# Streaming encoder trunk: the sample block's norm taken apart at the start of each FFN, and the second pair's own-block products issued first

## The chip, the cores and the metric

The kernel runs on one core of one Trainium2 chip. A core has five engines with queues of their own that work in order and meet through semaphores: TensorE (PE in the profile; PEld is its weight load), VectorE (DVE), ScalarE (ACT), GpSimd (POOL) and SyncE (SP), whose queue issues nearly all loads. The metric is the device time of one execution in microseconds (us).

## The reference

One inference step of a two-layer encoder for two groups of requests: a prompt of 512 rows and a sample of 8 x 16 = 128 rows, model width 1024, all float32. Layer 0 mixes with stick-breaking attention and gated linear attention, layer 1 with chunk-band softmax attention. After each mixer comes a norm and a SwiGLU FFN of hidden width 2816. The change lies in the two FFNs:

```python
def _rmsnorm(x, g):
    xf = x.astype(jnp.float32)
    y = xf * lax.rsqrt(jnp.mean(xf * xf, axis=-1, keepdims=True) + EPS)
    return (y * g.astype(jnp.float32)).astype(x.dtype)

def _swiglu(h, wg, wu, wd):
    return (jax.nn.silu(h @ wg) * (h @ wu)) @ wd
...
for layer in range(DEPTH):
    ...
    xp = xp + _swiglu(_rmsnorm(xp, norm_ffn_g[layer]), w_ffn_gate[layer], w_ffn_up[layer], w_ffn_down[layer])
    xs = xs + _swiglu(_rmsnorm(xs, norm_ffn_g[layer]), w_ffn_gate[layer], w_ffn_up[layer], w_ffn_down[layer])
```

## The kernel before

**Rows and columns.** Prompt and sample lie together as 640 rows, five blocks of 128; block 4 is the sample. The input of an FFN is held transposed in four tiles fT (256 columns of the model each, 640 rows). The FFN's rows fall in two halves of 320: n = 0 is blocks 0, 1 and half of 2, n = 1 the rest with the sample. The model's columns fall in two halves as well, so fT has four quarters: b11 and b21 (rows n = 0), b12 and b22 (rows n = 1).

**Products.** Each float32 product is three matmuls on parts of reduced precision: high x high, high x low, low x high. `split` (L286) makes the high part of a weight on ScalarE (`wh`, L289) and the low part on VectorE (`wl`, L290); four buffers of each exist, so splits run at most four products ahead. `product` (L688) is 12 matmuls of 128 x 320 (L692 to L694). `block` (L660) splits an operand in the same way (`xb` for a quarter, `xt` for a combined one; cast L664, difference L665), `comb` (L653) makes the combined operands t1 to t4 from quarters by VectorE differences (`xs`, L657).

**Pairs of matrices.** The FFN walks over the hidden width in groups of 6, 6, 6 and 4 tiles of 128. For every two tiles it takes a slice of the gate weights and then the same slice of the up weights; `fast_pair` (L670) is one such matrix of 1024 x 256, loaded as two halves `raw`. A matrix has four own blocks A. Usually it is computed with seven products in place of eight: `head` (b21 into py, b11 into px), `body` (t3 into pq; t2 on px; b22 into py; t1 on px), `tail` (t4 on pq). For t3, t2, t1 and b22 in the body, `weights` (L697) makes sums of own blocks on GpSimd: s3 and s1 come from own blocks, s2 from s1, s4 from s2. They lie in four buffers `sw`, and are split like weights.

**The start of an FFN.** The first pair (matrices 0 and 1 of group 0, gate and up) is computed plainly, with `part`: part(0) does the rows n = 0 with four products (b11, b21 for two output tiles), part(1) the rows n = 1 (b12, b22). So the first eight products need no sample rows. In the program's order (L779 to L799) stand: blocks b11 and b21, part(0) of matrix 0, part(0) of matrix 1, then `last_norm`, the norm of the sample block, then blocks b12 and b22, both part(1), the head of matrix 2, and the combinations and blocks t3, t1, t2, t4. `last_norm` is `norm_block` (L247) on xt[4]: `rstd_of` (L230) squares both halves of the rows on ScalarE with a sum (`sqj`, L235), takes the root as exp(-0.5 ln) with one correction step (L240 to L244), then both halves are scaled to `h` (L252; the first on VectorE, the second on GpSimd), transposed on TensorE (`tp`, L255) and written into fT with the gain (L261 on VectorE, L263 on ScalarE). The transposes are told to issue only after the last matmul of part(0) of matrix 1.

**What sets the order.** The program does not fix an engine's queue. A planner orders the instructions when the program is built, by their place in the program (or a priority given) and its own estimate of times; buffers of a ring with one tag are handed out by it as well. Six buffers with the tag `ws` serve, in an FFN, the squares' scratch `sqj`, the scaled rows `h`, the gate and up results `sg` and `up`, and the combined operands `xs`.

Of the kernel before, what the change touches and what calls it, by code (L numbers as in the profile page):

```python
# [13 lines left out]
ALU = mybir.AluOpType  # L14
PSUM = bass.MemoryType.PSUM

P = 128
# [38 lines left out]
def kernel(  # L56
# [8 lines left out]
    nc = tc.nc  # L65
# [35 lines left out]
    def tagged(tag, bufs, where="all"):  # L101
        def f(shape, name, dt=F32):
            return pools[where].tile(shape, dt, tag=tag, bufs=bufs, name=name)
        return f
# [5 lines left out]
    ws = tagged("ws", NWS)  # L110
# [12 lines left out]
    def pp(shape, name="pp"):  # L123
        return pps.tile(shape, F32, tag="pp", name=name)

    def za(shape, name="za"):
        return banks["za"].tile(shape, F32, tag="za", name=name)
# [23 lines left out]
    def plain():  # L151
# [14 lines left out]
        out=mask_a, in_=mask_a, pattern=[[-1, P]], compare_op=ALU.is_gt,  # L166
# [23 lines left out]
    def make_gla_masks(ch, nm):  # L190
# [23 lines left out]
        out=rowm, in_=rowm, pattern=[[-DS, DB]], compare_op=ALU.is_ge,  # L214
# [3 lines left out]
        out=rowm, in_=rowm, pattern=[[DS, DB]], compare_op=ALU.is_ge,  # L218
        fill=0.0, base=DS - 1, channel_multiplier=-1,
    )  # L220

    xs_flat = x_sample.rearrange("b t d -> (b t) d")

    def x_rows(src_p, src_s, b):
# [5 lines left out]
    def rstd_of(xt, sb=None):  # L230

        ss = small.tile([P, 2], F32, tag="ss", name="ss")
        for i in range(2):
            j = (sb or ws)([P, 512], "sqj")
            nc.scalar.activation(j, xt[i], AF.Square, scale=1.0 / 32.0, accum_out=ss[:, i:i + 1])  # L235
        v = small.tile([P, 1], F32, tag="rv", name="rv")
        r = small.tile([P, 1], F32, tag="rr", name="rr")
        a = small.tile([P, 1], F32, tag="ra", name="ra")
        V = nc.vector
        V.tensor_scalar(v, ss[:, 0:1], ss[:, 1:2], EPS, op0=ALU.add, op1=ALU.add)  # L240
        nc.scalar.activation(r, v, AF.Ln)
        last_exp[:] = [nc.scalar.activation(r, r, AF.Exp, scale=-0.5)]
        V.tensor_scalar(a, r, r, v, op0=ALU.mult, op1=ALU.mult)
        V.tensor_scalar(r, a, -3.0, r, op0=ALU.add, op1=ALU.mult)  # L244
        return r

    def norm_block(xt, gi, hT, b, sb=None, bank=None, after=None):  # L247
        r = rstd_of(xt, sb)
        for i in range(2):
            tp = (bank or za)([P, 4, P], "tp")  # L250
            h = (sb or ws)([P, 512], "h")
            scaled = (nc.vector, nc.gpsimd)[i].tensor_scalar(h, xt[i], r, -0.5, op0=ALU.mult, op1=ALU.mult)  # L252
            with tc.issue_after(after.ins) if after else nullcontext():
                for j in range(4):
                    nc.tensor.transpose(tp[:, j, :], h[:, j * P:(j + 1) * P], ident)  # L255
            for j in range(4):
                c = 4 * i + j
                if len(hT) == 4:
                    d = hT[c // 2][:, c % 2, b * P:(b + 1) * P]
                    if j % 2:  # L260
                        nc.vector.tensor_scalar(d, tp[:, j, :], gm[:, gi, c:c + 1], None, op0=ALU.mult)  # L261
                    else:
                        nc.scalar.activation(d, tp[:, j, :], AF.Copy, scale=gm[:, gi, c:c + 1])  # L263
                    continue
                H = hT[c][:, 0, b * P:(b + 1) * P]
                L = hT[c][:, 1, b * P:(b + 1) * P]
                g = gm[:, gi, c:c + 1]
                nc.scalar.activation(H, tp[:, j, :], AF.Copy, scale=g)
                nc.vector.scalar_tensor_tensor(
                    L, tp[:, j, :], g, H.bitcast(F32), op0=ALU.mult, op1=ALU.subtract)  # L270
        return scaled

    def new_hT(nm):
        return [t5([P, 2, NT], f"{nm}{c}", F32R) for c in range(8)]
# [395 lines left out]
    def fast_pair(W, c0, X, out):  # L670


        r = [pool.tile([P, 4, 256], F32, tag="raw", bufs=NRAW, name="raw"),
             pools["stage"].tile([P, 4, 256], F32, tag="rawf", bufs=2, name="raw")]
        for k in range(2):
            nc.sync.dma_start(r[k], W[512 * k:512 * k + 512, c0:c0 + 256].rearrange("(k p) n -> p k n", p=P))
        A = [[r[k][:, :, P * m:P * m + P] for k in range(2)] for m in range(2)]

        def part(n):

            for m in range(2):
                ps = za([P, 320], "pb")
                for k in range(2):
                    last = product(ps, A[m][k], (("b11", "b21"), ("b12", "b22"))[n][k], k == 0)
                out(m, n, ps, None)
            return last

        def product(ps, a, x, first=True):  # L688
            H, L = split(a, 4, P)
            for k in range(4):  # L690
                f = dict(skip_group_check=True)
                MM(ps, lhsT=H[:, k, :], rhs=X[x][0][k], start=(first and k == 0), stop=False, **f)  # L692
                MM(ps, lhsT=H[:, k, :], rhs=X[x][1][k], start=False, stop=False, **f)  # L693
                last = MM(ps, lhsT=L[:, k, :], rhs=X[x][0][k], start=False, stop=(k == 3), **f)  # L694
            return last

        def weights(a, b, op):  # L697
            t = sm_([P, 4, P], "sw")
            nc.gpsimd.tensor_tensor(t, a, b, op=op)  # L699
            return t  # L700
        st = {}

        def copy(ps):
            t = u2_([P, 320], "u2")
            nc.scalar.copy(t, ps)
            return t

        def head():
            st["Y"] = Y = pp([P, 320], "py")
            product(Y, A[0][1], "b21")  # L710
            st["X"] = Z = za([P, 320], "px")
            product(Z, A[0][0], "b11")
            st["P"] = copy(Z)

        def body():
            Z = st["X"]
            out(0, 0, st["Y"], st["P"])
            st["Q"] = Q = za([P, 320], "pq")
            s3 = weights(A[0][0], A[1][0], ALU.subtract)
            product(Q, s3, "t3")  # L720
            s1 = weights(A[1][0], A[1][1], ALU.add)
            s2 = weights(s1, A[0][0], ALU.subtract)
            product(Z, s2, "t2", False)
            q7 = copy(Q)
            st["U"] = copy(Z)
            Y = pp([P, 320], "py")
            s4 = weights(A[0][1], s2, ALU.subtract)
            product(Y, s4, "b22")
            product(Z, s1, "t1", False)
            out(0, 1, Z, copy(Y))  # L730
            out(1, 1, Z, q7)

        def tail():
            product(st["Q"], A[1][1], "t4", False)
            out(1, 0, st["Q"], st["U"])
        return head, body, tail, part

    def ffn(l, xt, fT, after, last_norm):
        X, comb, block = operand(fT)
        c0, silu = 0, []  # L740
        for gi, G in enumerate(GROUPS):
            gT, mats = [], []
# [33 lines left out]
            for i, (head, body, tail, part) in enumerate(mats):  # L776
                if gi == 0 and i == 1:
                    continue
                if gi == 0 and i == 0:  # L779


                    block("b11")
                    block("b21")
                    part(0)
                    last_norm(mats[1][3](0))
                    block("b12", gt_)
                    block("b22")
                    part(1)
                    mats[1][3](1)
                    mats[2][0]()  # L790
                    comb("t3", "b22", "b12")
                    block("t3")
                    comb("t1", "b12", "b11")
                    comb("t2", "b22", "t1")
                    block("t2")
                    block("t1")
                    comb("t4", "b21", "t2")
                    block("t4")
                    continue  # L799
                if gi or i > 2:  # L800
                    head()
                if i > 2 * (gi == 0):
                    mats[i - 1][2]()
                body()
            mats[-1][2]()
            if gi == len(GROUPS) - 1:
                with tc.issue_after(silu[-1].ins):
# [20 lines left out]
    hT = new_hT("hTa")  # L828
# [266 lines left out]
    for t in ORDER.split():  # L1095
        step(t)
    hT = new_fT("fT0")
    xt = mixer_end(w_out_ab[0], oT, oS, lambda b: x_rows(x_prompt, xs_flat, b), 1, hT, a_sample,
                   [FIRST + 99500 + 1000 * t for t in WHEN[0]])
# [9 lines left out]
        last_scaled[:] = [norm_block(xt[b], 2, hT2, b)]  # L1109
    stack.close()  # L1110
    with ffn_pools():
        ffn(0, xt, hT, after0, lambda mm: norm_block(xt[4], 1, hT, 4, after=mm))
    hT = hT2


# [53 lines left out]
    for half in range(2):  # L1169
# [7 lines left out]
        for p in range(p0 + 1, p0 + 4):  # L1177
            c_attend(p, *c_pair(p))

    hT = new_fT("fT1")  # L1180
    xt = mixer_end(w_out_c[0], oT, oS, lambda b: xd[b], 3, hT, lambda: (mixer_banks(*BANKS[2]), [c_sample(h) for h in range(2)]),
                   [FIRST + 299500 + 1000 * t for t in WHEN[1]])
# [11 lines left out]
        nc.sync.dma_start(dst, y)  # L1194
    stack.close()
    with ffn_pools():
        ffn(1, xt, hT, after1, lambda mm: norm_block(xt[4], 3, hT, 4, after=mm))


# [37 lines left out]
```

## Time and profile before

| what | value |
|---|---|
| time, median of 3 runs | 1778.29 us (1778.0, 1778.29, 1786.5) |
| the profiled execution: its time | 1781.72 us |
| the profiled execution: its span | 1780.0 us |
| granted clock of TensorE, mean over the span | 0.979 |
| HBM read, written | 175.75 MB, 14.29 MB |
| FFN 0 begins its first product at | 439.8 us |
| FFN 1 begins its first product at | 1321.0 us |

A row of a timeline gives start, duration, engine, line and operation, the tile written and those read, partitions x elements, a count, and in brackets how long the engine had been idle before and what ended that. A wait row gives the waiting line, what it waited for, the total in us, how often, and the longest. L numbers are lines of the kernel before.

### The profile page before, as it was taken

The numbers are of one execution on the slowest core, as the hardware profiler recorded it, in microseconds if no ns is written. First come the engines' busy times: TensorE is split into PE (matmuls) and PEld (weight loads), VectorE is DVE, ScalarE is ACT, GpSimd is POOL, SyncE is SP. The second block draws the span as 40 slices with busy tenths as digits, with TensorE's granted clock in tenths as the row PEclk, the third lists the DMA queues.
The fourth block names the chain that finished last, engine by engine and source line by source line (L and its number), as shares of the span: only waits on it lengthen the run. The fifth ranks groups of instructions, "written<-read, shape, count | busy, mean of one in ns | idle before, by whom it ended". The sixth has DMA issues, their size and how long they took to land.

```text
span 1780.0 us, 31737 instructions
## 1 busy us (share of the span) xinstructions
PE 1697.9 (95%) x12520; PEld 1522.9 (86%) x12520; DVE 1108.4 (62%) x2237; ACT 812.0 (46%) x1805; POOL 317.7 (18%) x339
## 2 busy tenths in 40 slices
PE   7999999998889999999999999999787999999997
PEld 7898997896788998989898889888567889899896
DVE  6466586765684765856555654755647837658465
ACT  6454435455552543534454433534536525335253
POOL 2000000000241413414110000001104224043130
PEclk9999998999899999999999999999998999999999
DMA  5311131574122222222343233368822313222212
GB/s 144 97 56 49 56 97 54 186 244 155 59 77 90 71 96 71 73 95 70 122 134 99 83 96 108 116 211 300 311 98 62 105 60 95 83 83 73 93 60 83
DMA packets 157173, 192.09 MB, mean 108 GB/s; under 512 B 12976, under 2 KB 109248, under 8 KB 157024
## 3 DMA queue, kind: packets, MB, share of 16 engines
q1 hardware_dynamic: 153440, 178.40, 30.8%
q0 software_dynamic: 3584, 11.67, 2.1%
q8 instruction: 98, 1.61, 0.4%
q14 instruction: 51, 0.42, 0.1%
HBM read 175.75 MB, written 14.29 MB: 107 GB/s over the span
## 4 chain that ended last, share of the span: by engine, by line
PE 82%; DVE 11%; ACT 3%; issue 2%; DMA 2%; SPq 0%; DVEq 0%; ACTq 0%
PE pn L323 6%; PE pn L325 6%; PE pn L324 6%; PE pw L304 5%; PE pw L305 5%; PE pw L306 5%; DVE wl L290 3%; PE px L692 3%; PE px L693 3%; PE px L694 3%; PE kttp L535 2%; PE py L694 2%; PE pm L356 2%; PE pm L359 2%; PE pm L358 2%
## 5 line engine op out<-in xcount | busy, mean ns | idle before, releaser
L290 DVE TENSOR_TENSOR wl<-raw,wh 128x512 fp32r<-128x512 f32 (+1 forms) x370 | 289.0, 788 | 251.0 <-ACT wh L289 248.5
L289 ACT CAST wh<-raw 128x512 fp32r<-128x512 f32 (+1 forms) x370 | 227.8, 618 | 377.7 <-PE pn L325 163.4
L699 POOL TENSOR_TENSOR sw<-raw 128x512 f32<-128x512 f32 x80 | 128.5, 1610 | 533.2 <-DMA raw<-in_w_ffn_gate_dram 298.2
L324 PE MATMUL pn<-wl,gT 128*128 128x512 f32 x440 | 171.2, 389 | 0.0
L289 ACT CAST wh<-sw 128x512 fp32r<-128x512 f32 x160 | 99.4, 621 | 154.9 <-PE px L693 64.4
L325 PE MATMUL pn<-wh,gT 128*128 128x512 f32 x440 | 169.3, 389 | 0.0
L323 PE MATMUL pn<-wh,gT 128*128 128x512 f32 x440 | 166.8, 389 | 0.0
L290 DVE TENSOR_TENSOR wl<-sw,wh 128x512 fp32r<-128x512 f32 x160 | 120.7, 758 | 52.6 <-ACT wh L289 41.4
L694 PE MATMUL py<-xb,wl 128*128 128x320 f32 x320 | 100.6, 314 | 9.2 <-DVE wl L290 9.2
L694 PE MATMUL pq<-xt,wl 128*128 128x320 f32 x320 | 98.8, 310 | 4.0 <-DVE wl L290 4.0
L692 PE MATMUL pq<-xt,wh 128*128 128x320 f32 x320 | 99.1, 310 | 2.2 <-ACT wh L289 2.2
L692 PE MATMUL px<-xt,wh 128*128 128x320 f32 x320 | 98.9, 309 | 0.0
L693 PE MATMUL pq<-xt,wh 128*128 128x320 f32 x320 | 98.9, 309 | 0.0
L693 PE MATMUL px<-xt,wh 128*128 128x320 f32 x320 | 98.9, 309 | 0.0
L694 PE MATMUL px<-xt,wl 128*128 128x320 f32 x320 | 98.9, 309 | 0.0
L693 PE MATMUL py<-xb,wh 128*128 128x320 f32 x320 | 98.8, 309 | 0.0
L692 PE MATMUL py<-xb,wh 128*128 128x320 f32 x320 | 98.8, 309 | 0.0
L325 PEld LDWEIGHTS pn<-wh,gT 128*128 128x128 f32 x440 | 82.6, 188 | 16.9
L324 PEld LDWEIGHTS pn<-wl,gT 128*128 128x128 f32 x440 | 82.6, 188 | 16.9
L323 PEld LDWEIGHTS pn<-wh,gT 128*128 128x128 f32 x440 | 82.3, 188 | 16.6
L304 PE MATMUL pw<-hTa,wh 128*128 128x320 f32 (+1 forms) x272 | 89.9, 331 | 0.0
L305 PE MATMUL pw<-hTa,wh 128*128 128x320 f32 (+1 forms) x272 | 88.9, 327 | 0.0
(329 smaller groups left out, 4721.5 us busy)
## 6 DMA issues: line engine op xcount, KB each, us to landing
raw<-in_w_ffn_gate_dram SPq DMA_DIRECT2D x44, 512.0 KB, 3.8
raw<-in_w_ffn_up_dram SPq DMA_DIRECT2D x44, 512.0 KB, 3.7
raw<-in_w_ffn_down_dram SPq DMA_DIRECT2D x44, 512.0 KB, 3.3
kr<-in_cache_c_k_dram SPq DMA_DIRECT2D x64, 256.0 KB, 5.4
vr<-in_cache_c_v_dram SPq DMA_DIRECT2D x16, 1024.0 KB, 7.0
raw<-in_w_in_ab_dram SPq DMA_DIRECT2D x24, 512.0 KB, 3.8
raw<-in_w_qkv_c_dram SPq DMA_DIRECT2D x24, 512.0 KB, 3.8
vr<-in_cache_a_v_dram SPq DMA_DIRECT2D x8, 1024.0 KB, 5.6
```

Source lines behind the costliest of these rows:

```text
L289: nc.scalar.copy(H, rawv)
L290: nc.vector.tensor_sub(L, rawv, H.bitcast(F32))
L304: MM(ps[i], lhsT=H[:, k % 4, :], rhs=hT[k][:, 0, s], start=(k == 0), stop=False)
L305: MM(ps[i], lhsT=H[:, k % 4, :], rhs=hT[k][:, 1, s], start=False, stop=False)
L306: MM(ps[i], lhsT=L[:, k % 4, :], rhs=hT[k][:, 0, s], start=False, stop=(k == 7))
L323: MM(ps[b], lhsT=lhs[k][:, 0, bs], rhs=H, start=(k == 0), stop=False)
L324: MM(ps[b], lhsT=lhs[k][:, 0, bs], rhs=L, start=False, stop=False)
L325: MM(ps[b], lhsT=lhs[k][:, 1, bs], rhs=H, start=False, stop=(k == K - 1))
L692: MM(ps, lhsT=H[:, k, :], rhs=X[x][0][k], start=(first and k == 0), stop=False, **f)
L693: MM(ps, lhsT=H[:, k, :], rhs=X[x][1][k], start=False, stop=False, **f)
L694: last = MM(ps, lhsT=L[:, k, :], rhs=X[x][0][k], start=False, stop=(k == 3), **f)
L699: nc.gpsimd.tensor_tensor(t, a, b, op=op)
```

## The change

`norm_block` is divided in `norm_rows` (square, root, scaling) and `norm_columns` (transposes and the write into fT). In each FFN the rows of the sample block are now asked for ahead of the first products, with both scalings on VectorE; the columns follow part(0) of matrix 0, their transposes behind its last matmul, and part(0) of matrix 1 comes after them. The head of matrix 3 is issued directly behind the head of matrix 2, ahead of the combinations. In the body of matrix 2 the sums s1, s2, s4 and the b22 product come first, and s3 with the t3 product after them. All other uses of the norm keep their order.

```diff
+    ROWS = (nc.vector, nc.vector)
...
-    def norm_block(xt, gi, hT, b, sb=None, bank=None, after=None):
+    def norm_rows(xt, sb=None, engines=None):
+
         r = rstd_of(xt, sb)
+        hs = []
         for i in range(2):
+            h = (sb or ws)([P, 512], "h")
+            scaled = (engines or (nc.vector, nc.gpsimd))[i].tensor_scalar(
+                h, xt[i], r, -0.5, op0=ALU.mult, op1=ALU.mult)
+            hs.append(h)
+        return hs, scaled
+
+    def norm_block(xt, gi, hT, b, sb=None, bank=None):
+        hs, scaled = norm_rows(xt, sb)
+        norm_columns(hs, gi, hT, b, bank)
+        return scaled
+
+    def norm_columns(hs, gi, hT, b, bank=None, after=None):
+
+        for i, h in enumerate(hs):
             tp = (bank or za)([P, 4, P], "tp")
-            h = (sb or ws)([P, 512], "h")
-            scaled = (nc.vector, nc.gpsimd)[i].tensor_scalar(h, xt[i], r, -0.5, op0=ALU.mult, op1=ALU.mult)
             with tc.issue_after(after.ins) if after else nullcontext():
...
-        def body():
+        def body(own=False):
+
             Z = st["X"]
             out(0, 0, st["Y"], st["P"])
             st["Q"] = Q = za([P, 320], "pq")
+            if own:
+                s1 = weights(A[1][0], A[1][1], ALU.add)
+                s2 = weights(s1, A[0][0], ALU.subtract)
+                s4 = weights(A[0][1], s2, ALU.subtract)
+                Y = pp([P, 320], "py")
+                product(Y, s4, "b22")
+                y = copy(Y)
             s3 = weights(A[0][0], A[1][0], ALU.subtract)
             product(Q, s3, "t3")
-            s1 = weights(A[1][0], A[1][1], ALU.add)
-            s2 = weights(s1, A[0][0], ALU.subtract)
+            if not own:
+                s1 = weights(A[1][0], A[1][1], ALU.add)
+                s2 = weights(s1, A[0][0], ALU.subtract)
             product(Z, s2, "t2", False)
             q7 = copy(Q)
             st["U"] = copy(Z)
-            Y = pp([P, 320], "py")
-            s4 = weights(A[0][1], s2, ALU.subtract)
-            product(Y, s4, "b22")
+            if not own:
+                Y = pp([P, 320], "py")
+                s4 = weights(A[0][1], s2, ALU.subtract)
+                product(Y, s4, "b22")
             product(Z, s1, "t1", False)
-            out(0, 1, Z, copy(Y))
+            out(0, 1, Z, y if own else copy(Y))
             out(1, 1, Z, q7)
...
+                    rows = last_norm[0]()
                     block("b11")
                     block("b21")
-                    part(0)
-                    last_norm(mats[1][3](0))
+                    last_norm[1](rows, part(0))
+                    mats[1][3](0)
                     block("b12", gt_)
                     block("b22")
                     part(1)
                     mats[1][3](1)
                     mats[2][0]()
+                    mats[3][0]()
                     comb("t3", "b22", "b12")
...
-                if gi or i > 2:
+                if gi or i > 3:
                     head()
                 if i > 2 * (gi == 0):
                     mats[i - 1][2]()
-                body()
+                body(gi == 0 and i == 2)
...
-        ffn(0, xt, hT, after0, lambda mm: norm_block(xt[4], 1, hT, 4, after=mm))
+        ffn(0, xt, hT, after0, (lambda: norm_rows(xt[4], engines=ROWS)[0],
+                              lambda rows, mm: norm_columns(rows, 1, hT, 4, after=mm)))
...
-        ffn(1, xt, hT, after1, lambda mm: norm_block(xt[4], 3, hT, 4, after=mm))
+        ffn(1, xt, hT, after1, (lambda: norm_rows(xt[4], engines=ROWS)[0],
+                              lambda rows, mm: norm_columns(rows, 3, hT, 4, after=mm)))
```

More of the change, by code (lines that the diff above doesn't have):

```diff
@@ L270, in norm_block @@
                     L, tp[:, j, :], g, H.bitcast(F32), op0=ALU.mult, op1=ALU.subtract)
-        return scaled
     def new_hT(nm):
```

## The prediction

> **What bounds the kernel now.** I read the page first: sections 1 and 4.
>
> ```profile
> PE 1697.9 (95%) x12520; PEld 1522.9 (86%) x12520; DVE 1108.4 (62%) x2237; ACT 812.0 (46%) x1805; POOL 317.7 (18%) x339
> ...
> PE 82%; DVE 11%; ACT 3%; issue 2%; DMA 2%; SPq 0%; DVEq 0%; ACTq 0%
> ```
>
> TensorE sets the time nearly everywhere. The change removes none of its products, so it can gain only where TensorE stands still or runs at a lower granted clock. Next the waits of TensorE, in the stretch where each FFN begins (FFN 0 near 440 us, FFN 1 near 1321 us).
>
> ```profile
> PE tp L255 <- DVE h L252: 5.0, 1, 5.0
> PE pb L693 <- DVE xb L665: 1.9, 1, 1.9
> PE pb L692 <- ACT xb L664: 1.3, 1, 1.3
> ...
> PE tp L255 <- DVE h L252: 4.9, 1, 4.9
> ```
>
> The first three are FFN 0 (454 to 470), the last is FFN 1. After the eight plain products of parts 0, TensorE waits 5 us for the scaled rows of the sample block, then for the low and high parts of what they feed. Windows put a size on it (columns: stretch, its length, busy time and count of PE, PEld, DVE, ACT and POOL, granted clock, DMA share, GB/s).
>
> ```profile
> 439.80:454.50 14.70, 14.70 (x99) 14.07 (x97) 8.15 (x15) 8.06 (x17) 0.00 (x0) 1.00 0.00 1
> 454.50:469.40 14.90, 6.76 (x25) 5.88 (x25) 9.93 (x15) 6.41 (x16) 6.36 (x5) 0.66 0.24 71
> ...
> 481.10:511.20 30.10, 24.75 (x163) 23.70 (x162) 29.37 (x38) 17.81 (x34) 20.63 (x8) 1.00 0.18 54
> ...
> 1335.50:1350.40 14.90, 6.83 (x28) 5.87 (x26) 9.95 (x15) 6.42 (x16) 6.36 (x5) 0.66 0.25 73
> ...
> 1362.00:1392.10 30.10, 24.69 (x163) 23.65 (x162) 29.36 (x38) 17.83 (x34) 20.64 (x8) 1.00 0.18 54
> ```
>
> Two things are to be seen. In 454.5 to 469.4 TensorE has 25 matmuls where the stretch before had 99, at a clock of 0.66. And in 481 to 511 (pair 2's bodies) VectorE has no idle left (29.37 of 30.10) and TensorE loses 5.35 us. The cadence, from the timeline of TensorE:
>
> ```profile
> 439.01 1.04 PE L255 MATMUL tp<-ident,h 128*128 128x128 f32 x8
> 439.80 0.39 PE L692 MATMUL pb<-xb,wh 128*128 128x320 f32 x1
> ...
> 459.57 1.94 PE L255 MATMUL tp<-ident,h 128*128 128x128 f32 x8 [4.95 <-DVE h L252]
> ...
> 466.29 0.47 PE L692 MATMUL pb<-xb,wh 128*128 128x320 f32 x1
> 466.55 0.47 PE L693 MATMUL pb<-xb,wh 128*128 128x320 f32 x1
> ...
> 469.42 0.31 PE L692 MATMUL pb<-xb,wh 128*128 128x320 f32 x1
> 469.56 0.31 PE L693 MATMUL pb<-xb,wh 128*128 128x320 f32 x1
> ```
>
> 0.26 us from one start to the next after the gap, 0.147 at full clock (14.70 / 99 in the stretch before is 0.148). A product of 12 matmuls is 1.76 us.
>
> Why are the rows so late? The timeline of the other engines:
>
> ```profile
> 439.21 0.69 DVE L626 TENSOR_TENSOR x<-x,ps 128x512 f32<-128x512 f32 x1 [6.18 <-PE ps L625]
> ...
> 441.14 2.17 ACT L289 CAST wh<-raw 128x512 fp32r<-128x512 f32 x4
> ...
> 455.03 0.42 ACT L763 COPY up<-pb 128x320 f32<-128x320 f32 x1
> 455.34 0.63 ACT L235 ACTIVATE sqj<-x 128x512 f32<-128x512 f32 x1
> ...
> 458.06 1.36 DVE L252 TENSOR_SCALAR h<-x,rr 128x512 f32<-128x512 f32 x1
> ...
> 1321.63 0.69 DVE L626 TENSOR_TENSOR x<-x,ps 128x512 f32<-128x512 f32 x1 [1.39 <-PE ps L625]
> ...
> 1323.23 0.62 ACT L289 CAST wh<-raw 128x512 fp32r<-128x512 f32 x1 [4.60 <-PE pb L693]
> ...
> 1323.89 0.69 DVE L290 TENSOR_TENSOR wl<-raw,wh 128x512 fp32r<-128x512 f32 x1 [1.57 <-ACT wh L289]
> ```
>
> The sample's x is final at 439.9, yet its first square starts at 455.34, right behind the last copy into `up`. The square's scratch comes from the ring `ws` that also gives `sg` and `up`, and it is asked for after them; I read the place in the queue as that order. So the norm is not late for want of data: it stands behind parts 0 in the program.
>
> **The change part by part.** *Norm taken apart.* Nothing is added: two squares, five one-column operations, two scalings, eight transposes, eight column writes stay. The second scaling goes from GpSimd to VectorE. The rows now stand ahead of all products, the transposes behind the first four (part 0 of gate) instead of the first eight.
>
> Are the rows in time? From square to last scaled row took 455.34 to 459.42, 4.1 us. In FFN 0 the x is final at 439.9 and ScalarE comes free near 441.2: the rows end near 445.3, or 447.4 behind the four casts of 441.14. Four products end at 439.8 + 7.04, near 447. In FFN 1 the x is final at 1322.3 and ScalarE idles until 1323.23: rows near 1326.5, four products end near 1328. No wait either way.
>
> Do the four products behind the transposes (7.04 us) cover the columns and the blocks b12 and b22? Before, from the transposes at 459.57 to the first low-part matmul near 465.6 were 6.0 us. They share the engines with four casts and four differences of splits, up to 4 x 0.69 = 2.8 us more. I take no wait; bound 0 to 1.8 us per FFN.
>
> What goes: stretch 454.5 to 469.4 holds 8 transposes (1.04 at full clock) and 17 matmuls (2.5): 3.5 of 14.9, so 11.4 us. FFN 1: 8 and 20, 4.0 of 14.9, so 10.9 us. Together **22.3 us**.
>
> What it costs at the start: in FFN 0 one square (0.63) on ScalarE and the scalings (1.36) on VectorE may stand ahead of the second product's split, whose cast runs only from 441.14, when the first product is nearly done. Bounds 0 and 2.0; I take 1.0, the middle, since no row tells which goes first. In FFN 1 ScalarE idles there: nothing.
>
> *Head of the fourth matrix issued ahead, b22 first in the second pair's first body.* No work is added. It moves 2 + 1 products, which need no combined operand, ahead of t3, t2, t1. Counted from the start of an FFN, products 1 to 16 are the plain parts, 17 to 20 now the two heads, 21 is b22, 22 t3. The three sums s1, s2, s4 must now all be made on GpSimd before the first body product, where s3 alone did. Loads: SP's queue keeps its order (gate of pair 2, then up of pair 2); the up halves must land two products earlier.
>
> ```profile
> 454.12 2.12 SPq L676 DMA_DIRECT2D raw<-in_w_ffn_gate_dram  x2
> 473.92 3.25 SPq L676 DMA_DIRECT2D raw<-in_w_ffn_up_dram  x2
> 475.95 0.42 ACT L750 COPY sg<-pb 128x320 f32<-128x320 f32 x1
> ...
> raw<-in_w_ffn_up_dram SPq DMA_DIRECT2D x44, 512.0 KB, 3.7
> ```
>
> The up halves were issued on either side of the end of product 12 (475.95 copies it out), the second by 477.2. In the new order product 12 ends at 439.8 + 1.0 + 1.04 + 21.1 = 463, so the second half is issued near 464.5 and there by 469; the fourth matrix's head begins after 18 products, at 473.5. Covered by some 4 us. The gate halves were issued by 456.2, at the end of product 8 (454.5); that now ends near 456, so they come 1.5 us later.
>
> When do the combined operands come? Their first casts waited as well:
>
> ```profile
> 477.93 0.46 ACT L772 CAST gT<-sg 128x320 fp32r<-128x320 f32 x1
> 478.29 1.35 ACT L664 CAST xt<-xs 128x640 fp32r<-128x640 f32 x2
> ```
>
> They came right behind the second gT tile, 2.3 us after product 12. This chain hangs on TensorE's own progress and so moves forward with it. It stays no better and no worse for the plain part of the change; VectorE's dense stretch after it stays too, with its 5.35 us. TensorE's waits in that stretch:
>
> ```profile
> PE py L694 <- DVE wl L290: 2.6, 3, 1.6
> PE pq L694 <- DVE wl L290: 2.0, 1, 2.0
> PE pq L692 <- ACT wh L289: 1.1, 1, 1.1
> ```
>
> None names a combined operand: all are splits of weights. The reorder gives cover for something that is not waited for by name, so I count it 0. Bounds: a gain of 5.35 + 5.41 if all these go, a loss as in the rivals.
>
> The sums are the risk:
>
> ```profile
> 460.43 1.27 POOL L699 TENSOR_TENSOR sw<-raw 128x512 f32<-128x512 f32 x1 [0.46 <-DMA raw<-in_w_ffn_gate_dram]
> ...
> 483.77 11.65 POOL L699 TENSOR_TENSOR sw<-raw 128x512 f32<-128x512 f32 x2 [18.92 <-DVE wl L290]
> 495.49 1.62 POOL L699 TENSOR_TENSOR sw<-sw,raw 128x512 f32<-128x512 f32 x1
> ```
>
> A sum takes 1.27 us alone; while VectorE has no gap two took 11.65, one of them thus being held for 9.1. The row of 460.43 began when the second gate half had come; in the new order that is near 462, and s1, s2, s4, s3 end near 463.3, 464.6, 465.8, 467.1 undisturbed. The b22 product comes at 439.8 + 1.0 + 1.04 + 20 x 1.76 = 477.0, t3 at 478.8. One held sum (9.1) is hidden, for s4 then ends at 474.9 and its split takes 0.62 + 0.69.
>
> The Trainium skill, page "SBUF — State Buffer", section "Who interferes with whom", says that a VectorE instruction with two SBUF inputs and a GpSimd one that reads SBUF lock each other out for a whole instruction. By it this order, which puts the sums beside VectorE's combinations, would hold several sums and end as the second or fourth rival does. The trace agrees with the lock at 483.77 (11.65 us for two) but not with a hold of every sum: the next took 1.62.
>
> **The sum.** -22.3 + 1.0 + 0 = -21.3 us. The profiled execution took 1781.72 us (span 1780.0, 1.72 around it) and would become 1760.4. It lies 3.4 us above the median of the runs, 1778.29; from the median I forecast **1757.0 us**.
>
> **The rivals.** 1. *The dense stretch loses its stalls as well*: 22.3 + 10.8 - 1.0 = 32.1, so 1746. For it: three plain products now lie ahead of the combined ones. Against: VectorE's 29.37 us of work there are the same. 2. *Two sums are held*: s4 ends at 465.8 + 18.2 = 484.0, its split 1.3 later, so TensorE waits 8.3 us per FFN: 16.6 of 21.3 given back, 1774. For it: VectorE gets its combinations nearer to the sums. Against: those hang on product 12 (463) and later, when the sums are nearly done. 3. *The rows do not come early*: the queue order is the planner's, and if it still puts the squares behind parts 0, or the transposes wait at product 4 as they did at 8, the gap only changes place: 1777. Against: the rows now ask for `ws` first. 4. *Slower: three sums are held*, in the same place: s4 ends at 465.8 + 27.3 = 493.1, TensorE waits 17.4 us per FFN at b22, 34.8 against 21.3 gained: 1792. It turns to a loss from 20.6 us of holding ahead of b22 (10.7 us of wait). Against: VectorE would have to run 27 us without a gap from 462, and in the stretch 454.5 to 469.4 it had 5 us of gaps.
>
> **How the numbers follow.** Forecast 0.57 (1750 to 1766); rival 1 0.13; rival 2 0.13; rival 3 0.10; rival 4 0.07. 0.5% is 8.9 us, about what a measurement of this kernel can tell from no change: faster is below 1769.4. Faster: 0.57 + 0.13 + 0.03 of rival 2, which may hold less, = 0.73; within: 0.10 + 0.10 = 0.20; slower 0.07. The range 1743 to 1774 takes in the forecast and rivals 1 and 2, with 0.83.
>
> **What would show it.** Right: squares of the sample near 440 and 1322, no wait of `tp` for `h` over 1 us, clock 1.00 in the first 30 us of each FFN. Wrong in the start: a wait for the second product's `wl` over 2 us. Rival 2 or 4: `py` waits for `sw` through its casts, with sums of several us on GpSimd near 460 to 480. Rival 1: the 30 us from pair 2's heads show TensorE idle for under 1 us. What would make the forecast wrong altogether is a planner that reorders other stages: then time moves outside 440 to 525 and 1321 to 1405.

## The result, and the profile after

The changed kernel takes **1767.01 us** (median of 6 runs, 1764.38 to 1770.24) where the kernel before takes 1782.14 us (6 runs, 1778.0 to 1786.5) beside it: a ratio of **0.9919, interval 0.9898 to 0.9939**. That is faster by more than 0.5%, as forecast, and 1767.01 lies inside the range. But the gain is some 15 us where the sum said 21.3.

The page of the kernel after, busy times and the shares of the chain that ended last:

```profile
PE 1699.9 (96%) x12520; PEld 1522.7 (86%) x12520; DVE 1114.4 (63%) x2239; ACT 810.8 (46%) x1805; POOL 310.9 (18%) x337
...
PE 82%; DVE 10%; issue 3%; ACT 3%; DMA 3%; POOL 0%; SPq 0%; DVEq 0%; ACTq 0%; POOLq 0%
```

Over the span little has changed but its length. The work is the same, so the start of the FFN has to be read by itself. First its waits of TensorE, FFN 0, 430 to 530 us:

```profile
PE px L706 <- ACT wh L303: 2.9, 1, 2.9
PE pb L708 <- DVE wl L304: 0.9, 2, 0.4
PE py L706 <- ACT wh L303: 0.7, 1, 0.7
PE pq L706 <- ACT wh L303: 0.7, 1, 0.7
PE pb L706 <- DVE rr L245: 0.5, 1, 0.5
```

The 5.0 us of `tp` for `h`, the 1.9 for `xb` and the 1.3 for `xb` are gone. (Lines have moved: the product's matmuls are now L706 to L708, `wh` L303, `wl` L304, the blocks L678 and L679, the sums L713, the transposes L270, the squares L236.) At the top stands a new one: 2.9 us of a `px` product for the high part of a weight. The windows of the same stretch, with the columns of the prediction's table:

```profile
439.95:449.57 9.62, 8.66 (x57) 7.92 (x56) 7.24 (x16) 5.71 (x15) 0.00 (x0) 1.00 0.01 2
449.57:462.00 12.43, 12.43 (x89) 12.42 (x87) 9.42 (x17) 8.81 (x19) 0.00 (x0) 1.00 0.22 61
462.00:475.15 13.15, 12.04 (x81) 11.51 (x79) 11.26 (x13) 8.61 (x16) 5.88 (x4) 1.00 0.36 104
475.15:486.70 11.55, 10.79 (x71) 10.27 (x71) 11.55 (x19) 9.82 (x20) 7.07 (x2) 1.00 0.16 47
486.70:496.24 9.54, 6.66 (x28) 6.40 (x29) 9.34 (x11) 1.84 (x4) 6.11 (x4) 0.64 0.38 110
```

The gap with its clock of 0.66 is gone: up to 486.7 the clock is 1.00 in every row. The last row is the loss that has come in its place: 28 matmuls, worth 4.1 us at 0.147, in 9.54 us, at a clock of 0.64. The rows of the sample block come early, as meant. The timeline, ScalarE's squares and TensorE's first product, its second, and the transposes:

```profile
434.00 0.63 ACT L236 ACTIVATE sqj<-x 128x512 f32<-128x512 f32 x1 [4.31 <-DVE x L640]
440.74 0.39 PE L706 MATMUL pb<-xb,wh 128*128 128x320 f32 x1
440.87 0.63 ACT L236 ACTIVATE sqj<-x 128x512 f32<-128x512 f32 x1
443.25 0.42 PE L706 MATMUL pb<-xb,wh 128*128 128x320 f32 x1 [0.51 <-DVE rr L245]
444.77 0.41 PE L708 MATMUL pb<-xb,wl 128*128 128x320 f32 x1 [0.45 <-DVE wl L304]
449.57 1.04 PE L270 MATMUL tp<-ident,h 128*128 128x128 f32 x8
```

The squares run at 434.0 and 440.9 instead of 455.3, and the transposes at 449.57 wait for nothing. The four products ahead of them take 449.57 - 440.74 = 8.83 us instead of 7.04: 1.79 lost, with two waits of the second product. The profile names `rr`, a column of the norm's root, as what ended the first; the product does not read it. What it needs is ScalarE's cast of its high part, which stands behind the square and the root there (it starts at 442.59 and takes some 0.6 us) and is ready at the same time. The second wait is for VectorE's split, which stands behind the two scalings (443.24 to 444.1).

To compare kernels I use the length of each FFN's beginning, from the first matmul of the first product to the issue of the first load of `w_ffn_down` (the loads keep their order, and in both kernels the windows of FFN 0 hold 356 matmuls and those of FFN 1 hold 355):

| | before | after | difference |
|---|---|---|---|
| FFN 0 | 439.80 to 509.94: 70.14 | 440.74 to 502.62: 61.88 | -8.26 |
| FFN 1 | 1321.03 to 1390.82: 69.79 | 1317.08 to 1377.52: 60.44 | -9.35 |

Together **-17.6 us**; the sum of the prediction said -21.3. The span is shorter by only 1780.0 - 1768.0 = 12.0 us, so 5.6 us more are lost elsewhere in this one profile; where they lie is seen below.

Where TensorE stops at `px`, the chain of waits in 480 to 497 us, followed back from its last matmul (start, length, what):

```profile
479.63 3.78 POOL sw L713
483.42 2.54 issue
485.96 1.86 POOL sw L713
...
487.89 1.74 POOL sw L713
...
489.65 0.63 ACT wh L303
...
490.32 0.63 PE px L706
490.95 0.27 PE px L707
```

It is GpSimd's sums, one behind the other, then the cast, then the matmul; and from there on 0.27 us a matmul. The operations behind it, from the timeline of GpSimd, VectorE and TensorE:

```profile
464.03 1.30 POOL L713 TENSOR_TENSOR sw<-raw 128x512 f32<-128x512 f32 x1 [31.95 <-DMA raw<-in_w_ffn_gate_dram]
...
468.51 1.56 POOL L713 TENSOR_TENSOR sw<-raw 128x512 f32<-128x512 f32 x1
479.63 8.18 POOL L713 TENSOR_TENSOR sw<-raw 128x512 f32<-128x512 f32 x2 [9.57 <-DVE wl L304]
485.16 5.14 DVE L679 TENSOR_TENSOR xt<-xs,xt 128x640 fp32r<-128x640 f32 x3
487.89 1.73 POOL L713 TENSOR_TENSOR sw<-sw,raw 128x512 f32<-128x512 f32 x1
490.32 0.63 PE L706 MATMUL px<-xt,wh 128*128 128x320 f32 x1 [2.88 <-ACT wh L303]
...
1354.85 8.18 POOL L713 TENSOR_TENSOR sw<-raw 128x512 f32<-128x512 f32 x2 [9.57 <-DVE wl L304]
...
1365.54 0.41 PE L706 MATMUL px<-xt,wh 128*128 128x320 f32 x1 [2.88 <-ACT wh L303]
```

The four sums of matrix 2 run undisturbed from 464.03 to 470.07. GpSimd then idles 9.57 us until a split sets a sum buffer free, and makes the sums of **matrix 3** while VectorE has no gap (11.55 of 11.55 in the window 475.15 to 486.70): 8.18 us for s3 and s1, while VectorE's three differences into `xt` take 5.14 us where 0.82 is the price of one. So s2 of matrix 3 ends at 489.62 and its t2 product waits. The last two rows are the same in FFN 1.

### The profile page after: what moved, and what is told of

It is laid out like the page before. It is cut to its first block, busy times and chain, and to the rows that moved or that the text cites. A ratio compares the mean times of both kernels' runs of the same rounds, so it can differ in the third digit from the quotient of the medians.

```text
span 1768.0 us, 31728 instructions
## 1 busy us (share of the span) xinstructions
PE 1699.9 (96%) x12520; PEld 1522.7 (86%) x12520; DVE 1114.4 (63%) x2239; ACT 810.8 (46%) x1805; POOL 310.9 (18%) x337
## 4 chain that ended last, share of the span: by engine, by line
PE 82%; DVE 10%; issue 3%; ACT 3%; DMA 3%; POOL 0%; SPq 0%; DVEq 0%; ACTq 0%; POOLq 0%
PE pn L337 6%; PE pn L338 6%; PE pn L339 6%; PE pw L318 5%; PE pw L319 5%; PE pw L320 5%; DVE wl L304 3%; PE px L706 3%; PE px L707 3%; PE px L708 3%; PE kttp L549 2%; PE py L708 2%; PE pm L370 2%; PE pm L373 2%; PE pm L372 2%
## 5 line engine op out<-in xcount | busy, mean ns | idle before, releaser
L304 DVE TENSOR_TENSOR wl<-raw,wh 128x512 fp32r<-128x512 f32 (+1 forms) x370 | 294.1, 803 | 233.3 <-ACT wh L303 231.0
L303 ACT CAST wh<-raw 128x512 fp32r<-128x512 f32 (+1 forms) x370 | 227.6, 618 | 362.8 <-PE pn L339 163.4
L713 POOL TENSOR_TENSOR sw<-raw 128x512 f32<-128x512 f32 x80 | 123.3, 1546 | 525.1 <-DMA raw<-in_w_ffn_gate_dram 334.2
L303 ACT CAST wh<-sw 128x512 fp32r<-128x512 f32 x160 | 99.4, 621 | 161.7 <-PE px L707 69.4
L304 DVE TENSOR_TENSOR wl<-sw,wh 128x512 fp32r<-128x512 f32 x160 | 121.2, 762 | 52.9 <-ACT wh L303 41.6
L708 PE MATMUL py<-xb,wl 128*128 128x320 f32 x320 | 100.7, 315 | 5.7 <-DVE wl L304 5.6
L706 PE MATMUL px<-xt,wh 128*128 128x320 f32 x320 | 100.6, 314 | 5.8 <-ACT wh L303 5.8
L706 PE MATMUL pq<-xt,wh 128*128 128x320 f32 x320 | 99.3, 310 | 1.4 <-ACT wh L303 1.4
L706 PE MATMUL py<-xb,wh 128*128 128x320 f32 x320 | 99.1, 310 | 1.3 <-ACT wh L303 1.3
L708 PE MATMUL px<-xt,wl 128*128 128x320 f32 x320 | 100.0, 312 | 0.0
L708 PE MATMUL pq<-xt,wl 128*128 128x320 f32 x320 | 99.0, 310 | 0.3 <-DVE wl L304 0.2
L318 PE MATMUL pw<-hTa,wh 128*128 128x320 f32 (+1 forms) x272 | 89.4, 329 | 0.0
L320 PE MATMUL pw<-hTa,wl 128*128 128x320 f32 (+1 forms) x272 | 88.5, 325 | 0.0
```

The lines of the kernel that those rows point to most:

```text
L303: nc.scalar.copy(H, rawv)
L304: nc.vector.tensor_sub(L, rawv, H.bitcast(F32))
L318: MM(ps[i], lhsT=H[:, k % 4, :], rhs=hT[k][:, 0, s], start=(k == 0), stop=False)
L320: MM(ps[i], lhsT=L[:, k % 4, :], rhs=hT[k][:, 0, s], start=False, stop=(k == 7))
```

## The experiments

Each edit is against the changed kernel. Ratios are to the kernel before on the same chip; "stretches" is the sum of the two beginnings, 139.93 before and 122.32 after. It does not end at quite the same work in every kernel: with the sums of matrix 3 on VectorE its two windows hold 363 and 362 matmuls (363 and 359 with the head ahead, 355 and 358 with the norm alone) where the changed kernel has 356 and 355. So the last column counts to the first matmul of the down product (`pn`), with 524 matmuls in each FFN in every kernel: 191.45 before, 174.19 after.

| kernel | ratio, interval | stretches, us | to the down product, us |
|---|---|---|---|
| changed kernel, first measuring | 0.9919 (0.9898 to 0.9939) | 122.32 | 174.19 |
| changed kernel, again | 0.9911 (0.9892 to 0.9929) | 122.67 | 174.33 |
| norm apart alone | 0.9890 (0.9864 to 0.9917) | 120.96 | 172.48 |
| order alone | 0.9991 (0.9976 to 1.0006) | 139.05 | 191.32 |
| norm and head ahead | 0.9894 (0.9871 to 0.9917) | 119.85 | 171.65 |
| norm and b22 first | 0.9893 (0.9871 to 0.9916) | 122.76 | 174.55 |
| five sum buffers | 0.9966 (0.9950 to 0.9981) | 124.84 | 175.96 |
| second scaling on GpSimd | 0.9891 (0.9876 to 0.9905) | 121.29 | 172.82 |
| sums of matrix 3 left out | 0.9860 (0.9845 to 0.9875) | 115.29 | 166.83 |
| sums of matrix 3 on VectorE | 0.9859 (0.9838 to 0.9879) | 119.40 | 168.16 |
| norm and head ahead, those sums on VectorE | 0.9855 (0.9839 to 0.9871) | 117.53 | 167.61 |
| norm apart alone, those sums on VectorE | 0.9871 (0.9855 to 0.9886) | 115.06 | 167.23 |

### The parts of the change alone

Norm taken apart, second pair in its old order:

```diff
-                    mats[3][0]()
...
-                if gi or i > 3:
+                if gi or i > 2:
...
-                body(gi == 0 and i == 2)
+                body()
```

> The norm taken apart, with the head of matrix 3 and the b22 product of matrix 2 back in their old places. Theory A (the reorder costs: it takes two products of cover from the sums of matrix 3, and the stall of 2.88 us before its t2 product with the slow clock after it follows from that): the gap of 11 us per FFN is gone, the stalls of the dense stretch are the old 5.4 us in place of about 7.7, so some 4 to 5 us faster than the changed kernel: 0.987 to 0.990 of the kernel before. Theory B (the reorder pays: without it TensorE reaches the combined operands too early): slower than the changed kernel by 3 us or more, 0.994 or above, with waits of pq or px for xt.

The new order with the norm as before:

```diff
-    ROWS = (nc.vector, nc.vector)
+    ROWS = (nc.vector, nc.gpsimd)
...
-                    rows = last_norm[0]()
...
-                    last_norm[1](rows, part(0))
-                    mats[1][3](0)
+                    part(0)
+                    mm = mats[1][3](0)
+                    last_norm[1](last_norm[0](), mm)
```

> The order of the second pair alone, with the norm whole and behind parts 0 as in the kernel before. Theory A: the gap of 11 us stays in each FFN, and the dense stretch loses up to 2.4 us more per FFN: 1.000 to 1.003 of the kernel before. Theory B: faster by 3 us or more, 0.998 or below, and the stalls of the dense stretch shrink.

The norm with one half of the order each: the head of matrix 3 ahead with the old body (only the last line of the first diff), and b22 first with the head where it was (the other two).

> The norm taken apart and the head of matrix 3 ahead, the body of matrix 2 in its old order. Theory A, with the head as the part that costs: as slow as the changed kernel, 0.991 to 0.993, with a stall of 2 us or more at a product of matrix 3 that wants a sum. If instead the b22 order costs: 0.987 to 0.990, no such stall. Theory B: between the two, 0.992 to 0.994.

> The norm taken apart and b22 first in the body of matrix 2, the head of matrix 3 behind that body as before. Theory A, with the head as the part that costs: 0.987 to 0.990, no stall over 2 us at matrix 3. If the b22 order costs: 0.991 to 0.993. Theory B: 0.992 to 0.994.

The norm apart is the whole gain, as far as the ratios tell: 0.9890 alone, 0.9991 for the order alone, whose interval takes in 1. The waits of TensorE at the start of FFN 0, order alone:

```profile
PE tp L270 <- DVE h L254: 4.1, 1, 4.1
PE px L706 <- ACT wh L303: 2.7, 1, 2.7
```

and norm alone:

```profile
PE py L708 <- DVE wl L304: 3.4, 4, 1.6
PE pq L708 <- DVE wl L304: 0.9, 1, 0.9
```

The single wait of `px` for `wh` comes with the head of matrix 3 ahead, whether the norm is moved (2.88 after, 3.05 with the old body) or not (2.74 in the order alone). Without that it is several waits of `wl`. The stretches hardly care: the head ahead is 1.1 us shorter than the norm alone, b22 first 1.8 longer, both together 1.4 to 1.7 longer, order alone 0.9 shorter than before. The order moves the stalls about; it doesn't remove them. The four ratios with the norm apart (0.9890 to 0.9919) can't be told apart by their intervals. So neither expectation came out whole: the stall of `px` comes with the head, as theory A has it, but without a cost that the ratios can tell, and the order alone fell between the two theories.

### The sums

Two theories were left for the 2.88 us: the sums of matrix 3 on GpSimd, held by VectorE and holding it; or VectorE simply being full. Sums of matrix 3 left out (an own block stands in the place of each):

```diff
-    def fast_pair(W, c0, X, out):
+    def fast_pair(W, c0, X, out, third=False):
...
+            if third:
+                return A[0][0]
...
-                    mats.append(fast_pair(w[l], c * P, X, o))
+                    mats.append(fast_pair(w[l], c * P, X, o, gi == 0 and len(mats) == 3))
```

> The changed kernel without the four GpSimd sums of matrix 3 in each FFN: its products take an own block in their place, so part of the output is not the reference's. Theory P (in the first pairs VectorE and GpSimd hold each other up at their shared access to the buffers, and the sums of matrix 3 come late by that): the wait of 2.88 us and the slow clock behind it go, VectorE's long differences (5.14 us for three) shrink to about 2.3, and the stretch from the first product to the first load of the down weights, 61.9 and 60.4 us in the changed kernel, falls to 56 to 58. Rival V (VectorE's own work, some 54 us of it, sets the end, with or without sums): the stretch stays at 59 or more, other waits for wl taking the place of the stall.

The same four sums made, but on VectorE:

```diff
-            nc.gpsimd.tensor_tensor(t, a, b, op=op)
+            (nc.vector if third else nc.gpsimd).tensor_tensor(t, a, b, op=op)
```

> The changed kernel with the four sums of matrix 3 on VectorE in place of GpSimd. Theory P: VectorE gets 4 x 0.69 = 2.8 us more and is no longer held by GpSimd there; no stall over 2 us, the stretch 57 to 60 us: 0.997 to 1.000 of the changed kernel or better. Rival V: 2.8 us more on the engine that sets the end: the stretch grows to 63 or more.

A fifth buffer for sums, so that GpSimd needn't wait 9.57 us before those of matrix 3:

```diff
-    sm_ = tagged("sm", 4, "stage")
+    sm_ = tagged("sm", 5, "stage")
```

> The changed kernel with five buffers for the sums in place of four, so that the first sum of matrix 3 need not wait for a buffer of matrix 2 (its wait of 9.57 us for wl). Rival B (the sums are late because their buffers come late): the first sum of matrix 3 starts near 472 in place of 479.6, the stall of 2.88 us at its t2 product shrinks below 1, the stretch falls by 3 us or more per FFN. Theory P: the sum starts earlier but is held or holds VectorE all the same; the stretch falls by less than 2 us.

Without the sums the stretches are 7.0 us shorter (122.32 to 115.29), 3.5 per FFN: that is what these eight instructions on an engine that is 18% busy cost TensorE. VectorE keeps all its own work, so its fullness alone does not make the stall. (A sum is held here too: the next one on GpSimd starts at 476.09 and takes 6.36 us, and three differences take 2.99. But no product waits for it.) Made on VectorE, the sums still give back 2.9 us by the stretches, and 6.0 of 7.4 us by the last column, which compares equal work. The timeline of VectorE, in the version with the head ahead and the sums on VectorE, where the changed kernel has its 5.14 us row:

```profile
483.38 1.55 DVE L679 TENSOR_TENSOR xt<-xs,xt 128x640 fp32r<-128x640 f32 x2
484.85 0.69 DVE L713 TENSOR_TENSOR sw<-raw 128x512 f32<-128x512 f32 x1
485.45 0.82 DVE L679 TENSOR_TENSOR xt<-xs,xt 128x640 fp32r<-128x640 f32 x1
```

Three differences and a sum end 2.9 us after they began. The Trainium skill, page "SBUF — State Buffer", section "Who interferes with whom", has the lock between a VectorE instruction with two SBUF inputs and a GpSimd one that reads SBUF go to whoever issues first. The runs agree on both sides: a GpSimd sum is held (6.36 us instead of 1.30), and VectorE's differences are as well (5.14 us for three instead of the 2.4 of these rows).

The fifth buffer makes the kernel slower than the changed kernel, 0.9966 against 0.9919 and 0.9911. Its timeline of GpSimd:

```profile
470.94 1.78 POOL L713 TENSOR_TENSOR sw<-raw 128x512 f32<-128x512 f32 x1 [0.94 <-DMA raw<-in_w_ffn_up_dram]
480.44 6.37 POOL L713 TENSOR_TENSOR sw<-raw 128x512 f32<-128x512 f32 x1 [7.72 <-DVE wl L304]
486.88 1.74 POOL L713 TENSOR_TENSOR sw<-sw,raw 128x512 f32<-128x512 f32 x1
```

s3 of matrix 3 comes early and unheld, but s1 then waits for the next buffer and is held (6.37) just the same, and two other waits (1.22 and 1.28 us) take the place of the 2.88. The stretches are 2.5 us longer; the rest of the loss lies in the later groups, 0.6 to 3.3 us in each by the loads of `w_ffn_down`. Why a fifth buffer costs there is not known.

### The start

The second scaling back on GpSimd, with the rest as changed:

```diff
-    ROWS = (nc.vector, nc.vector)
+    ROWS = (nc.vector, nc.gpsimd)
```

> The changed kernel with the second scaling of the sample rows on GpSimd as before. If the start cost of FFN 0 (1.2 us over the kernel before) is VectorE's: 0.4 us less of it. If GpSimd's row ends later than the first four products: a new wait of tp for h. I expect within 1 us of the changed kernel in either stretch.

The wait of 0.45 for `wl` at the second product goes, and the first four products take 8.43 us instead of 8.83, the 0.4 that was expected; the 0.50 put down to `rr` stays, and so does the stall of 2.88 us. The stretch of FFN 0 is 1.2 us shorter, a little more than expected. 0.9891 (0.9876 to 0.9905) can't be told from the changed kernel.

### The rest of the span, and what beats both

The changed kernel again, and two mixtures: norm and head ahead, or the norm alone, each with the sums of matrix 3 on VectorE (the diffs above put together).

> The changed kernel once more, on the same chip as the next two. What its first profile lost outside the two starts (3.1 us in the sample attention of layer 1, whose instructions stand in the same order in both kernels) is variation: the two stretches come again at 61.9 and 60.4 us, within 0.3, and the ratio to the kernel before comes out between 0.987 and 0.992. Rival: it belongs to the change; the stretch between the FFNs is again some 3 us longer than before.

> The norm taken apart and the head of matrix 3 ahead, the body of matrix 2 in its old order, the sums of matrix 3 on VectorE. Theory P (what is left of the stalls comes from VectorE and GpSimd holding each other up, and the order of the products moves it but does not take it away): stretches of 57 to 59 us, no stall over 2 us, 0.983 to 0.988 of the kernel before. Rival V (VectorE's work sets the end): 60 or more.

> The norm taken apart alone, the sums of matrix 3 on VectorE. Theory P: stretches of 58 to 60 us, 0.984 to 0.989 of the kernel before, level with the version with the head ahead within 1 us per FFN, so that the reorder is shown to be worth little. If the head's two products are a cover that counts: 2 us or more longer per FFN than with the head ahead.

The second measuring of the changed kernel gives 0.9911 (0.9892 to 0.9929), with the stretches 122.67 (61.81 and 60.86; the second is 0.4 us longer than the first time, just beyond what was expected). For the 5.6 us outside, the sample's attention of layer 1 is the largest piece. It lies between the two loads of gate weights for FFN 1 that SyncE issues ahead, at 1201.20 and 1313.16 us before, 1194.11 and 1309.21 after. Windows over just this piece, before and then after:

```profile
1201.20:1313.16 111.96, 97.20 (x1440) 75.14 (x1438) 60.78 (x175) 54.69 (x134) 11.22 (x41) 0.97 0.78 273
```

```profile
1194.11:1309.21 115.10, 100.32 (x1440) 76.18 (x1438) 60.52 (x175) 54.66 (x134) 11.19 (x41) 0.94 0.78 266
```

111.96 us before, 115.10 after: 3.1 of the 5.6. The 1440 matmuls are the same, but their order is not: the planner has moved transposes and products of this piece against each other. From the timeline of TensorE, behind the same eight transposes `tp`, before and then after:

```profile
1262.09 0.43 PE L542 MATMUL zs<-kt,qbdc 128*32 128x128 f32 x8
1262.45 1.53 PE L535 MATMUL kttp<-ident,kr 128*128 128x128 f32 x12
```

```profile
1255.08 0.64 PE L556 MATMUL zs<-kt,qbdc 128*32 128x128 f32 x16
1255.66 1.09 PE L549 MATMUL kttp<-ident,kr 128*128 128x128 f32 x8
```

Windows over the part that was reordered, between the same two places in the count of matmuls, before and then after:

```profile
1257.74:1290.90 33.16, 27.36 (x465) 20.30 (x461) 18.10 (x51) 16.12 (x38) 2.82 (x14) 1.00 0.83 282
```

```profile
1249.98:1288.17 38.19, 31.99 (x464) 23.00 (x460) 18.73 (x54) 16.05 (x37) 2.86 (x14) 0.87 0.75 246
```

This part alone is 5.0 us longer, at a clock of 0.87 instead of 1.00. Over the thirteen profiles its length goes with the order: in the six with the changed kernel's order (the changed kernel twice, head ahead, five buffers, second scaling on GpSimd, sums left out) it takes 35.10 to 38.26 us, in the seven with other orders 31.81 to 34.43. So the rival of the expectation came: the loss was there again in the second profile (114.38 for the piece, 37.55 for this part), and most of it seems to come with the change, by way of the planner. No run altered this order alone, so that is argued from the thirteen profiles, not shown. Scatter comes on top: with one and the same order the whole piece runs from 111.07 (head ahead) to 115.10. That is why I rest the sizes on the FFN starts, and the verdicts on the ratios; but the ratios take in this order too: norm alone, b22 first and the three kernels with sums on VectorE have another, shorter one.

Norm and head ahead with the old body, and the sums of matrix 3 on VectorE, beats both kernels: **0.9855 (0.9839 to 0.9871), median 1756.17 us**. Its interval lies wholly below both of the changed kernel's. It can't be told from norm alone with the same sums (0.9871, 0.9855 to 0.9886) nor from the changed kernel with them (0.9859), and at equal work the first two are level (167.61 and 167.23). Not all of the lead over the changed kernel is the sums': 6.6 us of it lie in the FFN starts, and the reordered part of the attention takes 32.10 us here where the changed kernel has 38.19 and 37.55.

## Why the prediction was right, and where its size was off

- **The gap, -22.3: right.** The queue order was the planner's, the cause was the place in the program (whether the ring `ws` held the squares as well was not tried apart), and the rows came early: squares at 434.0 and 440.9, no wait of `tp` for `h`, the clock at 1.00 through the first 30 us. Rival 3 falls with that, and the norm alone gives the whole gain.
- **The start, +1.0 in FFN 0 and 0 in FFN 1: right.** The four products lost 1.79 us. Before, the first eight lost 14.70 - 14.11 (96 matmuls of 0.147) = 0.59 over the same start, so the cost is 1.2. In FFN 1 they run without a gap (busy 7.45 of 7.45, 1317.08 to 1324.53). That the next four cover the columns and blocks was right too: 12.43 busy of 12.43.
- **The dense stretch stays, the reorder counts 0: this term was mis-sized.** By the steps, FFN 0 should have gained 11.4 - 1.0 = 10.4 and FFN 1 10.9; they gained 8.26 and 9.35. With 0.2 of it at the start, the dense stretches cost **3.5 us** more than before. As a check, FFN 0 by itself: 70.14 less what was lost before (0.59 + 11.4 + 5.35) is 52.8, so 61.88 - 52.8 = 9.1 are lost after: 1.79 at the start, 9.54 - 4.1 = 5.4 in the last window, and 1.8 in the single waits of 0.41, 0.70 and 0.69 us. The parts alone divide the 3.5: with the norm alone the stretches are 120.96 where 139.93 - 22.3 + 1.2 = 118.8 was due, so 2.1 come without any reorder, and the reorder adds 1.4 (1.7 in the second profile). I had read that none of the stalls named a combined operand, and that was so; but I took the stalls for a fixed sum that waits where it stands. In part they are made by sums and VectorE's stream meeting, and where they meet had moved. The trace before had it, in rows that I did not read together:

```profile
495.88 3.73 DVE L665 TENSOR_TENSOR xt<-xs,xt 128x640 fp32r<-128x640 f32 x2
499.54 0.68 DVE L290 TENSOR_TENSOR wl<-raw,wh 128x512 fp32r<-128x512 f32 x1
500.27 0.41 PE L694 MATMUL pq<-xt,wl 128*128 128x320 f32 x1 [2.00 <-DVE wl L290]
```

  Beside the sum of 495.49 and the one behind it two differences take 3.73 us, so the split comes late, and TensorE waits its 2.00 us for it. It is only a part: without the sums of matrix 3, 7.0 us go, about half of what the two dense stretches lose after the change (9.1 - 1.8 = 7.3 in FFN 0; in FFN 1, 69.79 - 10.9 - 5.41 = 53.5 is due and 60.44 was taken, 7.0). What makes the other half stays open; its waits are mostly for splits of weights.
- **Rival 2 was the right mechanism in the wrong place.** Sums were held, but not those of matrix 2: those were done by 470.07, three us behind my estimate of 467.1 and well ahead of their product. Held were those of matrix 3. So it had been before: the four sums of matrix 2 ended at 464.85, and the row of 483.77, behind its wait of 18.92 us for a buffer, is matrix 3's (one of its two sums took 9.82 us and the other 1.86, so one was held for 8.6 and not 9.1). I took its price and put it on matrix 2; the place of matrix 3's sums in the queue I had not followed: they wait for buffers until 479.55, when VectorE is full. They cost TensorE 3.5 us per FFN, not 8.3. Rival 4 is gone with it. Rival 1 stays out: what shortens the stalls is not the order but the sums' engine (7.4 us for the two starts by leaving them out, 6.0 by moving them).
- **From stretches to the median.** The stretches fell by 17.6, the medians by 15.1 (1782.14 - 1767.01). Against the gain stands the attention's new order, some 5 us in the first profile, and scatter the other way. That is the prediction's last sign, a planner that reorders other stages; it had no term in the sum.
- **How near the time came.** 1767.01 is 10.0 above the 1757.0 of the sum. The start value makes 3.9 of it (1778.29 in three runs, 1782.14 in six), the FFN starts 3.7, the rest 2.5. It lies in the range, but 1 us outside the 1750 to 1766 that the forecast gave itself, in the part that the rivals had added. The mechanism of the gain was right; that the time fell inside owes something to the width of the range.

## What to carry to other kernels

An order that puts a late step behind work it doesn't need shows as a wait with a slow clock behind it, and moving it in the program repays nearly what the windows say. But the stalls of a stretch where one engine is full are not a constant to carry over: follow every instruction that shares that engine's memory path, buffers included, to its new time. An engine at 18% may be the one that makes the full ones wait; giving its few instructions to a full engine can be the faster way. And read the order of stages that the change does not touch, since a planner may have moved them.

## What the runs showed of the hardware that I had not expected

- A sum of two 128x512 tiles on GpSimd takes 1.30 us alone and 6.36 beside VectorE's stream of differences and splits (9.82 before the change); VectorE takes 0.69 for the same sum. That VectorE's differences are lengthened too (5.14 us for three) was new to me: in the trace before I had read the hold on GpSimd's side only.
- A stall of 2.88 us is enough for the clock to fall. From 490.32 matmuls start every 0.267 us until 495.3, then every 0.147 again; the timeline of TensorE:

```profile
495.02 0.47 PE L707 MATMUL pq<-xt,wh 128*128 128x320 f32 x1
495.29 0.38 PE L708 MATMUL pq<-xt,wl 128*128 128x320 f32 x1
495.51 0.31 PE L706 MATMUL pq<-xt,wh 128*128 128x320 f32 x1
```

  Eighteen matmuls at 0.12 more are 2.2 us, not much less than the stall itself. In FFN 1 the same stall is followed by a dozen slow ones (clock 0.86 in the window 1365.54 to 1377.52). Before the change a stall of 2.00 us left the clock at 1.00. It is no matter of one length, though: with b22 first, a 14 us window of FFN 1 shows 0.90 where no wait in or just ahead of it is over 1.17:

```profile
1353.73:1367.73 14.00, 12.60 (x74) 11.90 (x74) 14.00 (x16) 6.62 (x13) 9.49 (x6) 0.90 0.25 77
```

  The Trainium skill, page "TensorE: Matmul & The Clock Gate", section "What's actually happening", puts the fall after an idle window of about 3.4 us that runs by a clock of its own; here less idle time sufficed.
